# Order of the first loads in a two-layer hybrid decoder kernel: x and the first weights first, parameter vectors on ScalarE's queue, late feature vectors behind the second weights

## The chip, the cores and the metric

The kernel runs on one core of a Trainium2 chip. The core has TensorE (PE, matrix products and transposes), VectorE (DVE), ScalarE (ACT), GpSimd (POOL) and SyncE (SP), each with its own instruction stream, and 16 DMA engines that carry out the transfers which SP, ACT and POOL issue. The metric is device microseconds for one execution; the time is the median of several runs. One more execution is recorded by the hardware profiler, and every duration here is read from that record.

## What is computed

The reference is a forward pass over 256 tokens of width 1024 through two layers. Only the beginning of the first layer matters here:

```python
h = rmsnorm(x, norm_mix[layer])
z = h @ w_in[layer]
cq, ckv, kpe, u_ssm, conv_a, conv_g, gates = jnp.split(z, IN_OFFSETS, axis=-1)
y_attn = mla_branch(cq, ckv, kpe, cos, sin, ...) @ w_o_attn[layer]
s = s5_branch(u_ssm, ssm_lam_re, ssm_lam_im, ssm_log_dt, ssm_b_re, ...)   # state-space branch
...
x = x + merged @ w_out[layer]
# layer 0: x + swiglu(...); layer 1: x + mixture of 8 experts, 2 per token
```

The state-space branch needs small parameter arrays (`ssm_lam_re`, `ssm_lam_im`, `ssm_log_dt`: 16 KB, 16 KB and 0.2 KB), the rotary tables need `positions` (1 KB), and norms and biases need nine feature vectors (1 to 8 KB each). The weights `w_in` come in pieces of 1 MB; x is 1 MB.

## The kernel before

Matrix products in full precision are made as three products of reduced-precision parts: a weight half `braw` (128x1024) is rounded by ACT to `bwh` (line 198), DVE subtracts to get the remainder `bwl` (line 199), and PE runs three matmuls per tile (lines 211 to 213). Where a projection is marked native, PE multiplies the raw weights directly (line 209), which needs neither split and takes longer per matmul. The projections of layer 0 run in the order of a plan: u0 (split), u1 (native), cq0 (split), then the pair conv a and g (native), gate2 (native), ckv0 (split), gate4 (native), gate0, gate5 and so on. Each 1 MB weight goes to one of two buffers (`load_next`, line 295); SP issues these loads.

Before u0 can start, x is squared and summed by ACT (line 671), DVE forms the inverse root by eight small steps (`nv`, `nr`), ACT and DVE scale one half of the tokens each into `xn` (lines 713, 714), PE transposes that sixteen times (line 731), and ACT and DVE split the result into `aH` and `aL` (lines 201, 202), scaled by `fv`, the feature vectors turned by a transpose (lines 387, 388). A parameter chain on DVE (`params`, from line 411) then forms tables from the transposed parameters (PE lines 426, 427 and 442): exponentials, sines, powers. It feeds the rotary table `tk` (PE line 517), the state-space output tables `rn` and `mout`, and input tables `ab`, which need the loads of `ssm_b_re` and `ssm_b_im` that ACT issues (line 602).

Three things set the order. The source gives a program order; a compile-time scheduler reorders each engine's stream within the dependences; on the chip each engine then runs its stream strictly in order. Transfers issued by SP and ACT count on eight shared completion semaphores, and a transfer that takes one again waits until the earlier transfer on it has landed: SP's third load waits for x in this way. In `mixer` (line 871) the old code issues x in `setup`, then the parameters (`params`, up to its first `yield`), then the feature vectors (`feature_rows`: the first two on SP, seven on ACT), and the first weight load comes when `top_up` asks for it.

Of the kernel before, what the change touches and what calls it, by code (L numbers as in the profile page):

```python
# [81 lines left out]
class Prog:  # L82
# [279 lines left out]


    def feature_rows(self):
        nc, io = self.nc, self.io
        spec = [("norm_mix", 8), ("norm_ffn", 8), ("q_norm", 2), ("kv_norm", 1), ("ssm_d", 4),
                ("ssm_b_glu", 4), ("conv_b", 4), ("conv_ln_g", 4), ("conv_ln_b", 4)]
        rows = [self.mixp.tile([128, 128], F32, tag=t, name="frows", bufs=1) for t in ("wr", "P1")]
        self.col = {}
        r = 0  # L370
        for name, n in spec:
            first = r < 32
            (nc.sync if first else nc.scalar).dma_start(
                rows[0][r:r + 2 * n] if first else rows[1][r - 32:r - 32 + 2 * n],
                io[name].rearrange("l (c p) -> (l c) p", p=128))
            for l in range(DEPTH):
                self.col[name, l] = r + l * n
            r += 2 * n
        self.nf = r
        self.fv = self.cp.tile([128, r], F32, name="fv")  # L380
        return rows

    def features(self, rows, ps, i):
        nc = self.nc
# [26 lines left out]
    def params(self, ps):  # L411

        nc, io = self.nc, self.io

        rows = self.scratch([64, 128])
        dtr = self.scratch([32, 2])
        pos_i = self.scratch([2, 128], I32)
        nc.sync.dma_start(rows[:32], io["ssm_lam_re"].rearrange("l (c g) p -> (l c) (g p)", g=2))
        nc.sync.dma_start(rows[32:], io["ssm_lam_im"].rearrange("l (c g) p -> (l c) (g p)", g=2))
        nc.sync.dma_start(dtr, io["ssm_log_dt"].rearrange("l (c g) -> (l c) g", g=2))  # L420
        nc.sync.dma_start(pos_i, io["positions"].rearrange("b (t p) -> (b t) p", p=128))
        yield 0
        dte = self.scratch([32, 2, 64])
# [1 line left out]
        p = ps.tile([128, 512], F32, name="aux", bufs=self.naux)  # L425
# [82 lines left out]
        for j in range(2):  # L508
            c, s = cs[:, 0, 32 + 16 * j:48 + 16 * j], cs[:, 1, 32 + 16 * j:48 + 16 * j]
# [361 lines left out]
    def mixer(self, l, wk, psp, raw=None):  # L871
        nc, io = self.nc, self.io
        if l == 0:
            params = self.params(psp)
            next(params)
            rows = self.feature_rows()
        if l == 0:
            xn = self.norm_stats(wk)
            self.features(rows, psp, 0)
# [6 lines left out]
            hH, hL = lambda c: H[:, c], lambda c: Lo[:, c]  # L886
        if l == 0:
            self.top_up()
            self.features(rows, psp, 1)
            for _ in params:  # L890
                pass
        mmt = lambda: psp.tile([128, 2, 256], F32, name="mm", bufs=2)
        aux = lambda: psp.tile([128, 512], F32, name="aux", bufs=1)

# [1101 lines left out]
```

## Time and profile before

| | us |
|---|---|
| median of 3 runs | 1732.92 (1732.33 to 1732.94) |
| the profiled execution | 1734.29 |
| its span, first to last instruction | 1732.6 |
| around the span | 1.69 |
| PE busy in the span | 1693.9 |
| mean granted TensorE clock | 0.994 |

PE is the busiest engine by far. Its idle time is therefore the thing to look for: where it sits, what ended it, and whether it stands at the beginning, where the change acts. Matmuls are pipelined, so the start of one to the start of the next is the time that one costs.

### The profile page before, as it was taken

The page shows a single profiled execution, that of the slowest core. Times are in us where ns is not written, and L with a number is a line of the kernel's source. Part 1 is how long each engine was busy: PE and PEld are TensorE (multiplying, and loading weights), DVE is VectorE, ACT ScalarE, POOL GpSimd, SP SyncE. Part 2 cuts the span into 40 slices and gives each one's busy share as a digit, 9 for nine tenths or more (in the row PEclk, how much of TensorE's full clock was granted, in tenths as well). Part 3 has the DMA queues.
Part 4 walks back from the last instruction along what each step waited for, and adds up shares of the span by engine and source line. Part 5 has one row for each costly group of instructions (what it writes and reads, how often), then busy time and mean ns, then how long its engine had stood idle before and what let it go on. Part 6 is the DMA issues. An engine that isn't in the chain of part 4 may idle for free.

```text
span 1732.6 us, 26103 instructions
## 1 busy us (share of the span) xinstructions
PE 1693.9 (98%) x9721; PEld 1458.9 (84%) x9721; DVE 1467.7 (85%) x2161; ACT 1170.1 (68%) x1534; POOL 44.9 (3%) x64
## 2 busy tenths in 40 slices
PE   7999999999999999999999999999999999999997
PEld 6899898999989999888888888888788888888875
DVE  7878887855578998689999999898988998989897
ACT  4545555664453665568887887787877887878775
POOL 2000000000000000000000000000000000100020
PEclk9999999999999999989999999999999999999999
DMA  5523355645644746679999799699999899998993
GB/s 157 150 82 99 117 182 177 176 147 182 195 147 153 242 147 221 235 279 378 362 369 395 274 383 395 250 394 395 342 393 393 299 393 392 340 394 320 395 394 140
DMA packets 262311, 471.27 MB, mean 272 GB/s; under 512 B 26832, under 2 KB 104816, under 8 KB 262176
## 3 DMA queue, kind: packets, MB, share of 16 engines
q1 hardware_dynamic: 245124, 455.70, 73.6%
q10 hardware_dynamic: 14732, 5.79, 1.3%
q0 software_dynamic: 2320, 8.03, 1.3%
q8 instruction: 78, 1.28, 0.3%
q14 instruction: 57, 0.47, 0.1%
HBM read 463.70 MB, written 5.78 MB: 271 GB/s over the span
## 4 chain that ended last, share of the span: by engine, by line
PE 93%; DVE 3%; ACT 2%; DMA 1%; issue 1%; ACTq 0%; SPq 0%; DVEq 0%
PE mm L212 19%; PE mm L211 19%; PE mm L213 19%; PE Y L212 6%; PE Y L213 6%; PE Y L211 6%; PE acc L213 2%; PE acc L212 2%; PE acc L211 2%; PE tr L1790 1%; PE mm L209 1%; PE bu L1237 1%; PE spare L629 1%; DVE bwl L199 1%; ACT bwh L198 1%
## 5 line engine op out<-in xcount | busy, mean ns | idle before, releaser
L198 ACT ACTIVATE bwh<-braw 128x1024 fp32r<-128x1024 f32 x248 | 261.1, 1058 | 201.5 <-PE mm L212 126.5
L199 DVE TENSOR_TENSOR bwl<-braw,bwh 128x1024 fp32r<-128x1024 f32 x248 | 301.4, 1223 | 103.5 <-ACT bwh L198 96.0
L211 PE MATMUL mm<-bwh,bxm 128*128 128x512 f32 x672 | 266.2, 396 | 0.0
L212 PE MATMUL mm<-bwl,bxm 128*128 128x512 f32 x672 | 264.6, 394 | 1.2 <-DVE bwl L199 1.2
L213 PE MATMUL mm<-bwh,bxm 128*128 128x512 f32 x672 | 262.5, 391 | 0.0
L212 PEld LDWEIGHTS mm<-bwl,bxm 128*128 128x128 f32 x672 | 126.3, 188 | 33.4 <-DVE bwl L199 9.4
L211 PE MATMUL mm<-aH,bwh 128*128 128x256 f32 x512 | 148.8, 291 | 0.4 <-ACT bwh L198 0.4
L213 PE MATMUL mm<-aH,bwl 128*128 128x256 f32 x512 | 146.4, 286 | 2.6 <-DVE bwl L199 2.6
L213 PEld LDWEIGHTS mm<-bwh,bxm 128*128 128x128 f32 x672 | 126.1, 188 | 25.9
L211 PEld LDWEIGHTS mm<-bwh,bxm 128*128 128x128 f32 x672 | 126.2, 188 | 25.2
L212 PE MATMUL mm<-aL,bwh 128*128 128x256 f32 x512 | 146.2, 286 | 0.0
L212 PE MATMUL Y<-bwl,bgates 128*128 128x512 f32 x336 | 133.5, 397 | 0.8 <-DVE bwl L199 0.8
L213 PE MATMUL Y<-bwh,bgates 128*128 128x512 f32 x336 | 132.8, 395 | 0.0
L211 PE MATMUL Y<-bwh,bgates 128*128 128x512 f32 x336 | 122.5, 400 | 0.0
L136 DVE SCALAR_TENSOR_TENSOR cacc<-zc,lc,cacc 128x256 f32<-128x256 f32 x240 | 108.7, 481 | 4.5 <-ACT cacc L1027 3.6
L211 PEld LDWEIGHTS mm<-aH,bwh 128*128 128x128 f32 x512 | 98.6, 193 | 3.8 <-issue 2.1
L213 PEld LDWEIGHTS mm<-aH,bwl 128*128 128x128 f32 x512 | 98.6, 193 | 3.1 <-DVE bwl L199 3.0
L212 PE MATMUL mm<-fL,bwh 128*128 128x256 f32 x352 | 99.4, 282 | 0.0
L213 PE MATMUL mm<-fH,bwl 128*128 128x256 f32 x352 | 99.3, 282 | 0.0
L211 PE MATMUL mm<-fH,bwh 128*128 128x256 f32 x352 | 99.3, 282 | 0.0
L212 PEld LDWEIGHTS mm<-aL,bwh 128*128 128x128 f32 x512 | 98.6, 193 | 0.2
L213 PE MATMUL mm<-baH,bxm 128*128 128x512 f32 x224 | 87.7, 391 | 0.0
(435 smaller groups left out, 4231.7 us busy)
## 6 DMA issues: line engine op xcount, KB each, us to landing
bmout<-in_moe_w SPq DMA_DIRECT2D x46, 1024.0 KB, 10.5
bbr<-in_moe_w SPq DMA_DIRECT2D x44, 1024.0 KB, 12.6
braw<-in_moe_w SPq DMA_DIRECT2D x44, 1024.0 KB, 13.9
braw<-in_w_in SPq DMA_DIRECT2D x36, 1024.0 KB, 5.3
braw<-in_ffn_w SPq DMA_DIRECT2D x31, 1024.0 KB, 5.1
bE<-in_moe_w SPq DMA_DIRECT2D x23, 1024.0 KB, 9.9
btoep<-in_moe_w SPq DMA_DIRECT2D x23, 1024.0 KB, 12.4
bq<-in_moe_w SPq DMA_DIRECT2D x23, 1024.0 KB, 14.8
```

The lines of the kernel that those rows point to most:

```text
L136: self.nc.vector.scalar_tensor_tensor(out, a, s, b, op0=op0, op1=op1)
L198: i = nc.scalar.activation(h, src, AF.Copy)
L199: j = nc.vector.tensor_tensor(l, src, h.bitcast(F32), op=OP.subtract)
L209: mm(out, wh, xh, start=start, stop=stop, skip_group_check=True)
L211: mm(out, wh, xh, start=start, stop=False, skip_group_check=True)
L212: mm(out, wh, xl, start=False, stop=False, skip_group_check=True)
L213: self.lastmm = mm(out, wl, xh, start=False, stop=stop, skip_group_check=True).ins
L629: nc.tensor.matmul(p[:, 32 * j:32 * j + 32], fx(self.bx[:, i, j]), c0m[:, i, 4 * u + j].rearrange("p a b -> p (a b)"), start=(i == 0), sto ...
L1237: nc.tensor.matmul(pb[:, i, c], self.minT[i][:, pair_at(8 * h + c)], U[:, 8 * h + c], start=True, stop=True)
L1790: nc.tensor.transpose(p[:, q * 128:(q + 1) * 128], s[:, q * 128:(q + 1) * 128], self.ident)
```

## The change

x still leads on SP. Straight behind it SP now issues the first 1 MB of weights (u0), then `positions`, then the second 1 MB (u1), then seven late feature vectors. ACT's queue, which had those seven, now issues `norm_mix`, `norm_ffn` and the three state-space parameters. The transposes of the late feature vectors come behind the parameter chain in program order.

```diff
     def feature_rows(self):
...
             first = r < 32
-            (nc.sync if first else nc.scalar).dma_start(
+            if r == 32:
+                yield rows
+            (nc.scalar if first else nc.sync).dma_start(
...
-        return rows
...
-        nc.sync.dma_start(rows[:32], io["ssm_lam_re"]...)
-        nc.sync.dma_start(rows[32:], io["ssm_lam_im"]...)
-        nc.sync.dma_start(dtr, io["ssm_log_dt"]...)
+        nc.scalar.dma_start(rows[:32], io["ssm_lam_re"]...)
+        nc.scalar.dma_start(rows[32:], io["ssm_lam_im"]...)
+        nc.scalar.dma_start(dtr, io["ssm_log_dt"]...)
         nc.sync.dma_start(pos_i, io["positions"]...)
...
     def mixer(self, l, wk, psp, raw=None):
         if l == 0:
+            self.load_next()
+            feats = self.feature_rows()
+            rows = next(feats)
             params = self.params(psp)
             next(params)
-            rows = self.feature_rows()
+            self.load_next()
+            for _ in feats:
+                pass
...
             self.top_up()
-            self.features(rows, psp, 1)
             for _ in params:
                 pass
+            self.features(rows, psp, 1)
```

The scheduler answers with other streams on every engine. From instruction 1036 of PE's 13450, 537 of DVE's and 194 of ACT's on, the order is that of before. Line numbers of the changed kernel are up to 7 higher. Three places matter.

On ACT, from the sum of squares on (`junk`): the names are as above, `h` is the unsplit copy for native projections. Before, then after:

```order
L671 ACT_TABLE_LOAD
L671 ACTIVATE junk,ss<-x 128x512 x4
L713 ACTIVATE xn<-x,nr 128x256 x2
L713 ACTIVATE xn<-x,nr 128x512
L201 ACTIVATE aH<-hp,fv 128x256
L198 ACTIVATE bwh<-braw 128x1024
L201 ACTIVATE aH<-hp,fv 128x256 x4
L198 ACTIVATE bwh<-braw 128x1024
```

```order
L422 DMA scr<-in_ssm_log_dt 32x2
L673 ACT_TABLE_LOAD
L673 ACTIVATE junk,ss<-x 128x512 x4
L198 ACTIVATE bwh<-braw 128x1024 x2
L715 ACTIVATE xn<-x,nr 128x256 x2
L715 ACTIVATE xn<-x,nr 128x512
L201 ACTIVATE aH<-hp,fv 128x256 x7
```

Both weight roundings of u0 moved ahead of `xn`.

On DVE, the end of the inverse root and what follows it (`nr` is its result):

```order
 L136 SCALAR_TENSOR_TENSOR rs_u<-rs_t 128x2
 L136 SCALAR_TENSOR_TENSOR nr<-rs_u,nr 128x2
-L388 COPY fv<-aux 128x32
-L714 TENSOR_SCALAR xn<-x,nr 128x256 x2
-L714 TENSOR_SCALAR xn<-x,nr 128x512
-L202 SCALAR_TENSOR_TENSOR aL<-hp,fv,aH 128x256
+L199 TENSOR_TENSOR bwl<-braw,bwh 128x1024
+L716 TENSOR_SCALAR xn<-x,nr 128x256 x2
+L716 TENSOR_SCALAR xn<-x,nr 128x512
+L390 COPY fv<-aux 128x32
```

The first weight remainder moved ahead of DVE's half of `xn`. The copy of `ssm_log_dt` stays in front of the whole inverse root, and the conversion of `positions` moved from its front into its middle.

On DVE again, some 50 us later, where ckv0's weights are split: `cacc` are the steps of the convolution, `ab` and `pz` products with the loaded `ssm_b_re` and `ssm_b_im`. Before, then after:

```order
L136 SCALAR_TENSOR_TENSOR zc<-mt,zc 128x2x256
L136 SCALAR_TENSOR_TENSOR cacc<-zc,lc,cacc 128x256 x5
L127 TENSOR_TENSOR ab<-lc,pz 128x1024
L136 SCALAR_TENSOR_TENSOR cacc<-zc,lc,cacc 128x256
L199 TENSOR_TENSOR bwl<-braw,bwh 128x1024 x2
```

```order
L136 SCALAR_TENSOR_TENSOR zc<-mt,zc 128x2x256
L136 SCALAR_TENSOR_TENSOR cacc<-zc,lc,cacc 128x256
L127 TENSOR_TENSOR ab<-lc,pz 128x1024
L136 SCALAR_TENSOR_TENSOR cacc<-zc,lc,cacc 128x256
L127 TENSOR_TENSOR pz<-lc,pz 128x1024
L199 TENSOR_TENSOR bwl<-braw,bwh 128x1024 x2
```

Four convolution steps left the front of `ab`, and one 128x1024 product with `ssm_b_im` now stands ahead of the two remainders of ckv0. In the same place ACT now issues the load of `ssm_b_re` ahead of its first convolution step instead of behind it.

## Rows read from the trace of the kernel before

**Rows 1.** Busy time by stretch: length, engines, granted clock, DMA share, GB/s.

```profile
0.00:62.00 62.00, 47.64 (x265) 41.43 (x265) 45.37 (x178) 28.66 (x53) 9.89 (x37) 1.00 0.55 154
62.00:140.00 78.00, 77.44 (x612) 71.87 (x613) 64.79 (x151) 39.96 (x73) 0.00 (x0) 0.98 0.41 121
```

**Rows 2.** Timeline of SP: start, length, what it issues.

```profile
0.81 0.88 SPq L351 DMA_DIRECT2D x<-in_x  x2
...
7.50 1.05 SPq L771 DMA_DIRECT2D braw<-in_w_in  x2
```

**Rows 3.** Single microseconds of the beginning: clock, DMA share, GB/s.

```profile
3.00:4.00 1.00, 1.00 1.02 415
...
8.00:9.00 1.00, 1.00 0.57 58
...
11.00:12.00 1.00, 1.00 1.10 377
```

**Rows 4.** Packets, MB, share: SP's queue (q1), ACT's (q10), 3.5-4; q10, 5-5.5.

```profile
q1 hardware_dynamic: 63, 0.20, 100.8%
q10 hardware_dynamic: 4, 0.00, 0.9%
...
q10 hardware_dynamic: 70, 0.02, 15.8%
```

**Rows 5.** The same for 321 to 322 us, in layer 0's feed-forward part.

```profile
q1 hardware_dynamic: 87, 0.36, 97.5%
q10 hardware_dynamic: 88, 0.01, 6.0%
```

**Rows 6.** One row of the chain of waits (start, length), then two of ACT's timeline.

```profile
1.68 4.26 DMA frows<-in_ssm_d
...
5.83 0.63 ACT L671 ACTIVATE junk<-x 128x512 f32<-128x512 f32 x1 [0.45 <-DMA x<-in_x]
...
12.89 1.06 ACT L198 ACTIVATE bwh<-braw 128x1024 fp32r<-128x1024 f32 x1 [0.17 <-DMA braw<-in_w_in]
```

**Rows 7.** Timeline of DVE, in brackets its idle time before and what ended it.

```profile
7.47 1.01 DVE L424 COPY scr<-scr 32x128 f32<-32x128 f32 x1 [6.26 <-DMA scr<-in_ssm_log_dt]
...
8.47 0.23 DVE L136 SCALAR_TENSOR_TENSOR nv<-ss 128x2 f32<-128x2 f32 x1
...
10.53 1.01 DVE L714 TENSOR_SCALAR xn<-x,nr 128x256 f32<-128x256 f32 x3
...
13.98 1.23 DVE L199 TENSOR_TENSOR bwl<-braw,bwh 128x1024 fp32r<-128x1024 f32 x1 [0.74 <-ACT bwh L198]
...
20.80 0.19 DVE L131 TENSOR_SCALAR scr<-aux 128x32 f32<-128x32 f32 x1 [0.70 <-PE aux L427]
```

**Rows 8.** Timeline of PE; a native matmul counts as two (x26 is 13).

```profile
11.09 3.40 PE L731 MATMUL hp<-ident,xn 128*128 128x128 f32 x16 [1.96 <-ACT xn L713]
14.24 0.37 PE L211 MATMUL mm<-aH,bwh 128*128 128x256 f32 x1
...
23.64 5.78 PE L209 MATMUL mm<-h,braw 128*128 128x256 f32 x26
29.06 0.47 PE L211 MATMUL mm<-aH,bwh 128*128 128x256 f32 x1
...
35.00 1.46 PE L209 MATMUL mm<-h,braw 128*128 128x256 f32 x6
37.27 0.59 PE L517 MATMUL aux<-ident,tk 128*128 128x128 f32 x2 [0.81 <-DVE tk L511]
```

**Rows 9.** The chain of waits from 52 us, then PE's timeline at 59 us.

```profile
54.37 4.98 DMA pz<-in_ssm_b_re
...
59.64 0.39 PE L211 MATMUL mm<-aH,bwh 128*128 128x256 f32 x1 [0.36 <-ACT bwh L198]
...
62.18 0.58 PE L213 MATMUL mm<-aH,bwl 128*128 128x256 f32 x1 [2.03 <-DVE bwl L199]
```

**Rows 10.** Busy time and granted clock (0.50) in the three microseconds behind that wait.

```profile
62.00:65.00 3.00, 2.82 (x13) 2.82 (x14) 3.00 (x5) 0.00 (x0) 0.00 (x0) 0.50 0.86 255
```

More of the change, by code (lines that the diff above doesn't have):

```diff
@@ L417, in params @@
         pos_i = self.scratch([2, 128], I32)
-        nc.sync.dma_start(rows[:32], io["ssm_lam_re"].rearrange("l (c g) p -> (l c) (g p)", g=2))
-        nc.sync.dma_start(rows[32:], io["ssm_lam_im"].rearrange("l (c g) p -> (l c) (g p)", g=2))
-        nc.sync.dma_start(dtr, io["ssm_log_dt"].rearrange("l (c g) -> (l c) g", g=2))
+        nc.scalar.dma_start(rows[:32], io["ssm_lam_re"].rearrange("l (c g) p -> (l c) (g p)", g=2))
+        nc.scalar.dma_start(rows[32:], io["ssm_lam_im"].rearrange("l (c g) p -> (l c) (g p)", g=2))
+        nc.scalar.dma_start(dtr, io["ssm_log_dt"].rearrange("l (c g) -> (l c) g", g=2))
         nc.sync.dma_start(pos_i, io["positions"].rearrange("b (t p) -> (b t) p", p=128))
```

## Prediction

> **What bounds the kernel now.** I read the busy times first: PE is busy for 1693.9 of the 1732.6 us of the span (the table of times), so only PE's idle time, or PE at a lower clock, can be won or lost. The busy time by stretch then says where that idle time is: 14.36 of the first 62 us (62.00 less 47.64), but 0.56 of the 78 us behind them [rows 1]. All that the change moves lies in this first stretch; from PE's instruction 1036 of 13450 on the streams agree again, so whatever PE has gained or lost by then it keeps to the end. The third view, the timelines of the engines, shows what PE waited for: the normalised x (first real transpose at 11.09, first matmul of u0 at 14.24), the rotary table at 37.27, and the remainder of ckv0's weights until 62.18 [rows 8, 9]. [...]
>
> **The change part by part.** First the loads. SP's two issues of x take 0.88 us, so the first weights go out at 1.69 instead of 7.50 [rows 2]. The second half of x lands at 5.83, where ACT stops waiting for it [rows 6]; a 1.05 MB load behind it, at the 377 to 415 GB/s of the full microseconds [rows 3], takes 2.5 to 2.8 us, so I put its landing at 8.6, an estimate. Bounds: 8.3, and 10.0 if it needs the 4.2 us that it took from its first bytes (about 8.7, since the microsecond from 8 moved only 58 GB/s) to 12.89 [rows 3, 6]. So its landing is some 4.3 us earlier; that is the gain meant.
>
> What of it reaches PE? u0 needs the normalised x as well, and that is not earlier: the squares end at about 8.1, as before, since they wait for x. Behind them three things stand in the way. (a) `ssm_log_dt` is now the fifth issue on ACT, at about 2.3. DVE's copy of it heads DVE's stream, in front of the whole inverse root. Before, its load went out behind x on SP, and the copy began at 7.47 [rows 7]. A small load issued on ACT's queue at 1.68 while x was moving landed only at 5.94 [rows 6], and the packets say why: 63 packets of SP's queue against 4 of ACT's from 3.5 to 4, and 70 of ACT's as soon as x was through [rows 4]. ACT's small loads came after what SP had issued ahead of them. Now the first weights are issued ahead of `ssm_log_dt` too. Bounds: it lands at 5.9 if only x holds it, at 8.7 behind the first weights, at 11.5 (8.7 and another 2.8) if the second weights hold it as well. I take 8.7, by the row that is nearest.
>
> [...]
>
> (b) With the copy at 8.7 and a small operation's 0.23 us [rows 7] the inverse root begins at 8.95 instead of 8.47 (9.7 if the copy again takes its 1.01). It took 2.06 to 10.53 [rows 7] and now has the conversion of `positions` within, 0.2: it ends at 11.2. `positions` is issued behind the first weights and lands with them, in time. (c) DVE then makes the first weight remainder before its half of `xn`: start to start that is some 1.14 (1.23 less an overlap of 0.09 with its neighbour) [rows 7]. So `xn` begins on DVE at 12.35, 1.8 later than before. ACT's two roundings, 1.06 each from 8.6, end at 10.7 and cost nothing, covered by the wait for the root; were the weights to land at 10.0 they would end at 12.1 and cost nothing still. PE's stream now begins with the second piece of `xn`: from about 12.9, and 15 of its 16 transposes at (14.24 less 11.09)/16 = 0.197 us [rows 8] make the first matmul of u0 15.85. **That is 1.6 later than 14.24.**
>
> Second, u0 and u1. Before, from 14.24 to 23.64 PE needed 9.40 us for 48 matmuls that come every 0.124 when nothing holds them (29.06 to 35.00, all 48 of cq0) [rows 8], since it waited for remainders and fitted 3 matmuls of u1 and four transposes between. Now both weight halves are split early: 48 x 0.124 = 5.95, three transposes 0.53, and about 0.2 for each of two changes of operand kind, 6.9. u0 ends at 22.75. u1's 16 native matmuls at (29.06 less 23.64)/13 = 0.417 [rows 8] make 29.4 against 29.06: **0.35 late**, so 1.25 of the 1.6 comes back.
>
> Third, the parameter chain. Its transposes stand earlier in PE's stream, behind 16 matmuls: its start on DVE is at 15.85 + 1.9 + 0.6 = 18.35 instead of 20.80 [rows 7]. From there to the first transpose of `tk` it took 16.5 (37.27 less 20.80) [rows 7, 8], and one `aL` of 0.4 has come in: 35.3. But that transpose has moved forward as well, to within cq0, where PE arrives at 29.4 + 39 x 0.124 = 34.2, so PE waits 1.1 where it waited 0.81. What is then left of the work that was done at 37.86 before: the pair of transposes and a change 0.8, nine matmuls 1.1, three natives 1.3, the late feature vectors 0.25, together 3.45. That makes 38.75: **0.9 late**.
>
> Fourth, ckv0. PE would arrive 0.9 later, but it waits there anyway, so DVE decides. `ssm_b_re` is now issued ahead of ACT's convolution step, right after `mt`: not 54.37 but about 53.5 (PE ends the 16 natives ahead of `mt` at about 59.28 less the 16 of gate2, 6.7, which is 52.6, and is 0.9 late). With its 4.98 [rows 9] it lands at 58.5; if the load of ckv0's weights holds it as long as before, at 60.2. Before, the remainder was ready 2.8 after `ab` began, at 59.35. Now the product with `ssm_b_im` stands between, 1.14 more: 3.9, so PE goes on at 62.4 to 64.1 instead of 62.18. I take the middle and a little less, **1.0 late**, and with it the same low clock behind the wait. The four convolution steps moved behind, 4 x 0.4, and the remainders of gate0 now behind the tables cost nothing as long as PE has 13 natives and 90 transposes and small matmuls to run meanwhile; where that cover ends, up to 1.5.
>
> The sum against the profiled execution is 1734.29 + 1.0 = 1735.3. That execution is 1.37 above the median, so the forecast is 1732.92 + 1.0 = **1733.9**.
>
> **The rivals.** *`ssm_log_dt` lands with x* (5.9). The root begins at 8.1, all of the above up to `tk` is 0.85 earlier, PE's delay at 37.86 turns into a lead of nearly nothing, and ckv0 gives -0.6 to +1.1: 1732.9. For it speak [rows 5], against it [rows 4].
>
> *`ssm_log_dt` lands behind both weights* (slower). If ACT's small packets wait until SP's stream has a gap, DVE stands until 11.5, the root starts 2.8 later than in the forecast, and nothing in the parameter chain can give it back: 1733.9 + 2.8 = 1736.7. From a landing at 11.2 on it is slower by over 0.2%. Against it: the second weights wait for a semaphore that x frees, so they are issued after it, and in [rows 4] a queue's turn went by who was first.
>
> *The wait for ckv0's remainder disappears* (faster). If `ssm_b_re`, issued earlier, lands before 57, the remainder is there when PE comes, and the 0.36 + 2.03 us go, and with them the low clock, where 13 matmuls took 2.82 [rows 10] instead of 13 x 0.124: 1.2. That is -3.6, with a start between -0.4 and +0.9: 1728.9 to 1730.2. Against it: the load took 4.98 beside ckv0's own weights, and DVE has an operation more to do.
>
> *Nothing arrives at PE*: the streams differ but every wait ends where it did, 1732.9.
>
> **How the numbers follow.** About 0.2%, 3.5 us, is what a measurement of this kernel can tell from no change. Chances: forecast 0.45 (its own range 1732.9 to 1735.8), `ssm_log_dt` with x 0.27 (1731.5 to 1734.0), behind both weights 0.08, the wait gone 0.08, of which 0.05 lies beyond 0.2%, nothing arrives 0.12. So faster 0.05, within 0.2% 0.87, slower 0.08. The range 1731.0 to 1736.0 takes in the forecast, the first rival and the last, and leaves out the two at the ends.
>
> **What would show it.** In the changed profile: the first `bwh` at about 8.6 and not 12.89; DVE's copy of `ssm_log_dt` at 8.7, `nv` at 8.95, DVE's `xn` at 12.35, the first u0 matmul at 15.85; no wait of PE for `bwl` in u0; the first transpose of `tk` at 35.3 after a wait of about 1.1; the wait for ckv0's `bwl` ending between 62.4 and 64.1 and the clock at 0.50 behind it. The forecast is wrong if the copy starts near 6 or near 11.5, if `ssm_b_re` lands before 57, or if PE shows new waits over 1.5 us between 65 and 200.

## The result, and the profile after

The changed kernel takes 1743.18 us (median of six runs, 1741.41 to 1744.86) where the kernel before, run beside it, takes 1734.23: **1.0052 times as long, 95% interval 1.0041 to 1.0063**. It is 9 us slower, and the prediction, 1733.9 with a range up to 1736.0, did not hold. One execution of e1 below took 5931 us and is left out of its figures. The profiled execution took 1744.22 with a span of 1742.4.

The busy times by stretch, in the columns of [rows 1], show where to look. First the kernel after, then the stretch from 140 us on of before, which [rows 1] did not reach:

```profile
0.00:62.00 62.00, 47.43 (x265) 41.77 (x265) 42.37 (x174) 28.57 (x53) 9.84 (x37) 1.00 0.53 150
62.00:140.00 78.00, 75.35 (x595) 69.79 (x596) 65.42 (x153) 39.74 (x73) 0.00 (x0) 0.98 0.39 118
140.00:175.00 35.00, 34.02 (x252) 31.07 (x251) 23.92 (x64) 12.78 (x24) 4.24 (x8) 0.85 0.25 75
```

```profile
140.00:175.00 35.00, 34.78 (x275) 31.03 (x274) 29.43 (x90) 18.12 (x41) 4.25 (x8) 1.00 0.21 63
```

The first 62 us, where the prediction looked for everything, differ by 0.2 us of busy time. From 62 to 140 PE idles 2.1 us more. From 140 to 175 it is nearly as busy as before but finishes 23 matmuls fewer, at a mean granted clock of 0.85: that place stands in no part of the prediction.

A ledger makes this exact. PE does the same work in both kernels, so the same group of matmuls can be looked up in both traces; how much later it starts is what has been lost by then. The columns are single profiled executions (the experiments are told below).

| place in before's trace, us | what starts there | after | e1 | e2 | e8 | e12 |
|---|---|---|---|---|---|---|
| 62.18 | ckv0, behind the wait | +1.69 | +1.78 | +0.12 | +0.10 | +0.10 |
| 120.60 | `aux<-u`, second half | +2.05 | +2.20 | +0.18 | -0.94 | +0.30 |
| 154.25 | `aux<-ys`, first half | +2.27 | +2.41 | +0.19 | -0.94 | +0.29 |
| 162.96 | `aux<-ys`, second half | +6.60 | +2.41 | +4.10 | -0.95 | +1.80 |
| 191.96 | `mm<-br` | +8.58 | +2.81 | +4.92 | -0.51 | +2.75 |
| 212.95 | `mm<-br` | +9.51 | +3.46 | +5.84 | +0.22 | +2.56 |
| 357.45 | `spare<-c0m` | +10.60 | +4.29 | +6.42 | +1.04 | +3.12 |
| 1719.09 | `aux<-bgates`, last stage | +9.85 | +3.30 | +6.53 | +1.48 | +2.30 |

So after is 2 us late when the first state-space tables are through, and 6.3 us more go between 154 and 192. The rest is small; part of it is again a lower clock, behind the wait for `ssm_c_im` near 302 us (0.86 from 300 to 312 in e1 and e2, 1.00 in before and after) and from 357 us on in after (0.55 from 357 to 360). A lower clock comes in one execution and not in another (0.68 from 158 to 174 in after, 1.00 in e5, the same kernel again), so a column of this table holds some microseconds of chance.

**The beginning** went nearly as predicted. Rows of after that answer to [rows 7], [rows 6] and [rows 8], on DVE, ACT and PE:

```profile
8.05 0.42 DVE L426 COPY scr<-scr 32x128 f32<-32x128 f32 x1 [6.84 <-DMA scr<-in_ssm_log_dt]
8.55 0.16 DVE L136 SCALAR_TENSOR_TENSOR nv<-ss 128x2 f32<-128x2 f32 x1
...
11.64 1.01 DVE L716 TENSOR_SCALAR xn<-x,nr 128x256 f32<-128x256 f32 x3
```

```profile
9.41 2.00 ACT L198 ACTIVATE bwh<-braw 128x1024 fp32r<-128x1024 f32 x2 [0.89 <-DMA braw<-in_w_in]
```

```profile
15.59 0.53 PE L211 MATMUL mm<-aH,bwh 128*128 128x256 f32 x1
...
29.33 0.47 PE L211 MATMUL mm<-aH,bwh 128*128 128x256 f32 x1
...
35.51 0.30 PE L519 MATMUL aux<-ident,tk 128*128 128x128 f32 x1 [1.16 <-DVE tk L513]
```

**At ckv0** (answering to [rows 9]) PE goes on at 63.87 instead of 62.18. Its two waits in after, then DVE ahead of them in after, then in before:

```profile
60.80 0.39 PE L211 MATMUL mm<-aH,bwh 128*128 128x256 f32 x1 [0.70 <-ACT bwh L198]
...
63.87 0.58 PE L213 MATMUL mm<-aH,bwl 128*128 128x256 f32 x1 [2.56 <-DVE bwl L199]
```

```profile
59.92 1.23 DVE L127 TENSOR_TENSOR ab<-lc,pz 128x1024 f32<-128x1024 f32 x1 [0.94 <-DMA pz<-in_ssm_b_re]
61.07 0.48 DVE L136 SCALAR_TENSOR_TENSOR cacc<-zc,lc,cacc 128x256 f32<-128x256 f32 x1
61.46 1.22 DVE L127 TENSOR_TENSOR pz<-lc,pz 128x1024 f32<-128x1024 f32 x1
62.60 2.35 DVE L199 TENSOR_TENSOR bwl<-braw,bwh 128x1024 fp32r<-128x1024 f32 x2
```

```profile
60.51 0.48 DVE L136 SCALAR_TENSOR_TENSOR cacc<-zc,lc,cacc 128x256 f32<-128x256 f32 x1
60.91 2.35 DVE L199 TENSOR_TENSOR bwl<-braw,bwh 128x1024 fp32r<-128x1024 f32 x2
63.18 0.48 DVE L136 SCALAR_TENSOR_TENSOR cacc<-zc,lc,cacc 128x256 f32<-128x256 f32 x1
63.57 1.22 DVE L127 TENSOR_TENSOR pz<-lc,pz 128x1024 f32<-128x1024 f32 x1
```

The second product (`pz`) has come ahead of the remainders (`bwl`) that PE is waiting for.

**At 160 us** the same has happened in another place. `P` holds the state-space branch's outgoing states, which the `y` matmuls take. In after, its last operation stands behind the bias additions `u`, which themselves wait 1.48 us for PE's transposes; in before it stood ahead. DVE after, then before:

```profile
156.86 0.69 DVE L127 TENSOR_TENSOR P<-P,T 128x512 f32<-128x512 f32 x1
159.02 0.87 DVE L136 SCALAR_TENSOR_TENSOR u<-u,fv,aux 128x256 f32<-128x256 f32 x2 [1.48 <-PE aux L1327]
159.81 0.68 DVE L127 TENSOR_TENSOR P<-P,wi 128x512 f32<-128x512 f32 x1
```

```profile
154.59 0.69 DVE L127 TENSOR_TENSOR P<-P,T 128x512 f32<-128x512 f32 x1
155.19 0.69 DVE L127 TENSOR_TENSOR P<-P,wi 128x512 f32<-128x512 f32 x1
156.75 0.48 DVE L136 SCALAR_TENSOR_TENSOR u<-u,fv,aux 128x256 f32<-128x256 f32 x1 [0.88 <-PE aux L1320]
```

PE has two `y` matmuls that need no final `P`, and then stands. Two microseconds after it has gone on, its matmuls lengthen (each counts as two). PE after, then its busy time and clock around this place:

```profile
159.18 0.39 PE L1254 MATMUL y<-P,mout 128*128 128x63 f32 x2
160.55 0.43 PE L1255 MATMUL y<-P,mout 128*128 128x63 f32 x2 [0.98 <-DVE P L127]
...
162.38 0.39 PE L1254 MATMUL y<-P,mout 128*128 128x63 f32 x2
162.61 0.51 PE L1255 MATMUL y<-P,mout 128*128 128x63 f32 x2
```

```profile
158.00:174.00 16.00, 15.02 (x100) 13.28 (x98) 7.01 (x23) 4.75 (x12) 4.24 (x8) 0.68 0.12 33
```

Single two-microsecond stretches of after show a granted clock of 0.50 from 164 to 172, 0.68 in the stretch before and 0.76 behind. So the 6.3 us between 154 and 192 are, by difference, the wait, 1.2 with what surrounds it (e5 below, which has the wait alone, loses 1.19 between the two `aux<-ys`), 0.4 up to 192 that e1 and e5 lose as well at clock 1.00 (0.40 and 0.43), and some 4.7 of half clock.

### The profile page after: what moved, and what is told of

Read it like the earlier page. It is cut to its first block, busy times and chain, and to the rows that moved or that the text cites. A ratio compares the mean times of both kernels' runs of the same rounds, so it can differ in the third digit from the quotient of the medians.

```text
span 1742.4 us, 26100 instructions
## 1 busy us (share of the span) xinstructions
PE 1700.8 (98%) x9721; PEld 1464.8 (84%) x9721; DVE 1466.8 (84%) x2161; ACT 1171.0 (67%) x1534; POOL 44.8 (3%) x64
## 4 chain that ended last, share of the span: by engine, by line
PE 92%; DVE 4%; ACT 2%; DMA 2%; issue 1%; ACTq 0%; SPq 0%; DVEq 0%
PE mm L212 19%; PE mm L211 19%; PE mm L213 19%; PE Y L212 6%; PE Y L213 6%; PE Y L211 6%; PE acc L213 2%; PE acc L212 2%; PE acc L211 2%; PE tr L1797 1%; PE mm L209 1%; DVE bwl L199 1%; ACT bwh L198 1%; PE bu L1244 1%; PE spare L631 1%
```

## The experiments

Theory A: what counts is not the loads but the order that the builder gave VectorE because of them, at two places where PE waits for it, together with the low clock behind such a wait. Rivals: the low clock belongs to the narrow matmuls there (B), or the loss is the beginning's and only shows up later (C). All ratios are to the kernel before in runs on the same chip. "Pin" means an issue-order edge between two instructions of one engine, with no wait.

**The order at P, undone and done alone.** e1 is the changed kernel with `P` ahead of `u`; e2 is the kernel before with the opposite pin.

```diff
# e1, in turn_out of the changed kernel
-                tt(hi, hi, wi, OP.add)
+                last = tt(hi, hi, wi, OP.add)
+                if h and l == 0:
+                    for q in range(2):
+                        self.tc.add_manual_dep(sg["bias", 0, q].ins, last.ins.name, ...)
...
# e2, in turn_out of the kernel before
-                tt(hi, hi, wi, OP.add)
+                if h and l == 0:
+                    with self.tc.issue_after(sg["bias", 0].ins):
+                        tt(hi, hi, wi, OP.add)
+                else:
+                    tt(hi, hi, wi, OP.add)
...
```

> The changed kernel with one pin: in layer 0 VectorE issues the last addition of the second state half's outgoing rotation (the write of P, which TensorE's y matmuls wait for) ahead of the first half's two bias additions (u), as it stood in the kernel before. Theory A (of the 9 us, 5.9 come from this order: 1.0 us in which TensorE waits for P at 160 us, and 4.9 us at a granted clock of 0.50 behind it): no wait of TensorE for P, granted clock 1.00 from 150 to 190 us, time 5 to 6.5 us below the changed kernel, 1737 to 1738 where before stands at 1734.2. Rival B (the low clock comes from what TensorE does there, narrow matmuls and transposes, and not from the wait): the wait goes, the low clock stays, 1742 to 1743. Rival C (the 9 us were lost at the beginning and the later places only follow): 1743.

> The kernel before with the opposite pin and nothing else of the change: the write of P is issued behind the two bias additions. Theory A: TensorE waits 1.0 to 2.0 us for P near 158 us, the granted clock falls to 0.50 for some 10 us behind that, time 4.5 to 7 us above before (1739 to 1741 where before stands at 1734.2). Rivals B and C: a wait of about 1 us without a lower clock, or no effect: 1734 to 1735.5.

e1: 1.0026 (1.0015 to 1.0036), 1737.0 beside 1732.5. e2: 1.0037 (1.0024 to 1.0051), 1740.8; six of its eight executions lie between 1740.6 and 1741.2, the other two at 1736.2 and 1737.7. Busy time and clock of 158 to 174 us, e1 and then e2, and e2's wait on PE:

```profile
158.00:174.00 16.00, 15.39 (x127) 13.43 (x124) 11.91 (x44) 9.22 (x25) 4.25 (x8) 1.00 0.15 41
```

```profile
158.00:174.00 16.00, 15.36 (x99) 13.29 (x99) 9.34 (x32) 7.52 (x19) 4.25 (x8) 0.79 0.04 4
```

```profile
158.46 0.43 PE L1248 MATMUL y<-P,mout 128*128 128x63 f32 x2 [0.98 <-DVE st L131]
```

In e1 the `y` matmuls are the same and run at clock 1.00, with no wait; in e2, which has no part of the change, both the wait and the low clock appear (the profile names DVE's neighbouring `st`, but the write of `P` is what ends at 158.4). B and C fall for this place. The price is a little under what I had written for e1: half of the 9 us, not two thirds.

**Which part of the change makes the order.** e3 calls the two weight loads early and changes nothing else; e4 has the other parts without that.

```diff
# e3, in mixer of the kernel before
+            self.load_next()
             params = self.params(psp)
             next(params)
             rows = self.feature_rows()
+            self.load_next()
# e4: the queue lines of the change's diff, and
-            self.features(rows, psp, 1)
             for _ in params:
                 pass
+            self.features(rows, psp, 1)
```

> The kernel before with one part of the change alone: the two weight loads are called ahead of and right behind the parameters' loads, on the queue that they had; feature vectors and parameters stay on their queues. The builder then orders VectorE around 160 us as in the changed kernel. Theory A: the low clock at 160 us is there, time 6 to 10 us above before (1740 to 1744). Rival C (the queues and the late feature vectors cost most): within 2 us of before.

> The kernel before with the other two parts: parameters and early vectors on ScalarE's queue, late vectors on SyncE's, and the late vectors' transposes behind the parameters'; the weight loads are called where they were. VectorE's order around 160 us stays that of before. Theory A: no low clock at 160 us, time from 1 us below to 1.5 us above before (1733 to 1736). Rival C: most of the 9 us, 1740 to 1743.

e3: 1.0051 (1.0036 to 1.0067); e4: 1.0010 (1.0000 to 1.0020). The early call of the weight loads alone brings a loss as large as the whole, and the order at `P` and the 0.98 us wait with it (until 162.10). But its profile shows clock 1.00 there, against what I expected, and its loss is in part another: e3 is 3.20 late at ckv0 already, where after is 1.69 late, since its small loads now stand behind the weights on SP's queue (feature vectors at PE at 11.34 instead of 8.85, transposes of x at 13.42 instead of 11.09).

**Is the low clock always there?** e5 is the changed kernel again; e9 lengthens e2's wait by pinning `P` behind the next product (`lt`) too.

> The changed kernel once more, for a second profile of it. Theory A in its present form: the wait of TensorE for P at 160 us (0.98 us) stands in every execution, since it comes from the order of the program, and the low clock behind it (4.7 us lost in the first profile) in most executions but not in all: the times fall into two groups, near 1741.5 and near 1744.5. Rival D (the low clock belongs to the place, not to chance): the same low clock at the same place, 5 to 6 us, and one group of times.

> The kernel before with the write of P pinned behind the first GELU product (lt) as well as behind the bias additions: the wait of e2_before_sub_last made longer. Theory A: TensorE waits 2.3 to 3.0 us for P near 158 us instead of 0.98; the low clock behind a wait of this length comes in nearly every execution, as behind the 1.6 to 2.6 us waits at ckv0: time 6.5 to 9 us above before (1739 to 1742 where before stands at 1732.6), one group of times. Rival D (the low clock there has nothing to do with how long TensorE waited): 2 us above e2_before_sub_last and the same two groups.

e5: 1.0048 (1.0034 to 1.0061), in two groups (1738.8 to 1740.8, and 1743.1 and 1743.5). The same wait, and this time no low clock behind it:

```profile
161.57 0.43 PE L1255 MATMUL y<-P,mout 128*128 128x63 f32 x2 [0.98 <-DVE P L127]
```

```profile
158.00:174.00 16.00, 14.80 (x133) 12.78 (x131) 11.08 (x37) 7.58 (x19) 4.24 (x8) 1.00 0.20 60
```

So the low clock at `P` is not certain, as the expectation of e5 said. e9 did not do what I wanted: the builder drew the attention's `sc` matmuls forward, and PE waited twice (0.78 and 0.68) instead of once for longer. Its profile has no low clock there and was its fastest execution (1736.5); the others lie between 1739.0 and 1744.1 at mean granted clocks of 0.992 to 0.988. Ratio 1.0042 (1.0030 to 1.0054). Whether a longer wait makes the low clock surer stays open at this place.

**The order at ckv0.** e6 gives the changed kernel before's order at both places. e8 puts ckv0's remainders ahead of all products, e12 does so without e1's pin, and e7 does it in the kernel before.

```diff
# e7, e8, e12, in ssm_inp (self.kv: the remainders of ckv0's two halves)
...
+            pin = (lambda: self.tc.issue_after(self.kv[0])) if l == 0 else nullcontext
-            self.tt(ab[:, o], fr, x, OP.mult)
+            with pin():
+                self.tt(ab[:, o], fr, x, OP.mult)
             yield 1.1
-            self.tt(tmp, fi, y, OP.mult)
+            with pin():
+                self.tt(tmp, fi, y, OP.mult)
# e6: kv[1], and the first ab product left free
```

> The changed kernel with two pins, so that VectorE keeps the order of before at both places: P ahead of the bias additions at 160 us (as e1_sub_first), and both rounding remainders of ckv0's weights (bwl, L199) ahead of the second product of the input matrices' build (pz, L127) at 61 us. Theory A: TensorE goes on with ckv0 at 62.6 instead of 63.9 us, 1.0 to 1.5 us less than e1_sub_first, that is 1 to 3 us above before (1733.5 to 1735.5 where before stands at 1732.5). Rival E (the time gained at ckv0 is waited for again at the input matrices' transposes, 74 to 87 us, whose chain on VectorE then ends later): within 0.5 us of e1_sub_first, 1737.

> The kernel before with one pin: both remainders of ckv0's weights go on VectorE ahead of all products of the input matrices' build. In the trace of before the first remainder starts at 60.9 us, 1.4 us after its rounding has ended (59.5), behind a 1.22 us product and a cacc addition. Theory A (order on VectorE at the places where TensorE waits is what counts): TensorE's wait of 2.0 us there falls to about 0.9 us and the time to 1 to 3 us below before (1729.5 to 1731.5 where before stands at 1732.5; the larger figure if the low clock behind the wait goes too). Rival E: the products come 1.5 to 2.3 us later, TensorE waits for their transposes from 68 us on, and the time is that of before within 0.5 us or up to 2 us longer.

> The changed kernel with P ahead of the bias additions and both remainders of ckv0's weights ahead of all products of the input matrices' build. Theory A: 1.5 to 3 us less than e1_sub_first, near before (1732 to 1735 where before stands at 1732.5). Rival E: within 0.5 us of e1_sub_first, 1737.

> The changed kernel with ckv0's remainders pinned ahead (as e8_after_kv_first) but with P left behind the bias additions: the fourth corner beside the changed kernel (neither pin), e1_sub_first (P alone) and e8_after_kv_first (both). If the two places add up (theory A): the wait of 0.98 us for P is there, ckv0's two waits are 0.9 and 1.0 us as in e8_after_kv_first, and the time is 3 to 5 us above e8_after_kv_first, 1.0020 to 1.0035 times before (some 1736.5 to 1739 where before stands at 1733). If P's cost hangs on the late ckv0: near e8_after_kv_first, 1.0005 to 1.0012.

| kernel | P ahead of u | ckv0's remainders first | ratio to before (95%) |
|---|---|---|---|
| after; e5 | no | no | 1.0052 (1.0041 to 1.0063); 1.0048 (1.0034 to 1.0061) |
| e1 | yes | no | 1.0026 (1.0015 to 1.0036) |
| e12 | no | yes | 1.0027 (1.0015 to 1.0038) |
| e8 | yes | yes | 1.0007 (0.9998 to 1.0016) |

The two places add up, as far as the intervals can tell. `P` ahead is worth 0.0020 to 0.0024, some 3.5 to 4.2 us; ckv0's remainders first 0.0019 to 0.0023, some 3.3 to 4.0. Each of these prices is a difference of two ratios and good to about 2.5 us, an estimate from their intervals; the two together, e5 less e8 on one chip, are 0.0041, 7.1 us. With both pins, the loads moved as the change moves them cost 1.2 us, which the interval does not tell from nothing. PE's waits at ckv0 in e8, and the clock of 60 to 70 us in e8 and in e12:

```profile
60.80 0.38 PE L211 MATMUL mm<-aH,bwh 128*128 128x256 f32 x1 [0.91 <-ACT bwh L198]
...
62.28 0.39 PE L213 MATMUL mm<-aH,bwl 128*128 128x256 f32 x1 [0.97 <-DVE bwl L199]
```

```profile
60.00:70.00 10.00, 8.23 (x61) 7.81 (x62) 10.00 (x14) 4.44 (x8) 0.00 (x0) 1.00 0.71 212
```

```profile
60.00:70.00 10.00, 8.22 (x51) 7.95 (x52) 10.00 (x14) 3.43 (x7) 0.00 (x0) 0.83 0.71 211
```

The waits are the same in both to 0.02 us (0.93 and 0.97 in e12), yet e12 has the low clock behind them and e8 has not; by 120.60 that is 1.24 us between them in the ledger.

e6 went against theory A: 1.0037 (1.0023 to 1.0051), no better than e1. PE went on at 62.94, 0.9 earlier than after, but then stood 1.21 us until 97.81 for `U` and was 3.2 late at 154. That is the kind of loss that its rival E names, though at another place and larger. So the order of before at these two places does not bring its time back by itself: with these pins a wait came up elsewhere. e7 missed as well: 0.9998 (0.9989 to 1.0007). With the products held back, the builder put further `cacc` additions in front of the remainders, which started at 60.67 instead of 60.91; nothing was left to gain.

**Does the beginning count?** e10 is e8 with the norm's products ahead of the first weight split. e11 is e4 with e7's pin, as a candidate for a faster kernel.

```diff
# e10, in top_up, for u0's first half
+                    with self.tc.issue_after(self.last[0]), self.tc.issue_after(self.last[1]):
+                        self.ready.append((key,) + self.wsplit(src))
```

> The kernel of e8_after_kv_first with the norm's products (xn) ahead of the first rounding of the weights on both ScalarE and VectorE, which undoes the prediction's step (c) at the beginning. If the beginning counts: first transposes near 11.2 instead of 12.3 us and 0.5 to 1 us less at the end (1734 where e8_after_kv_first had 1734.8). If it is hidden, as the parameters' chain on VectorE (tk, 35.3 us) holds TensorE next: the gain is waited for at tk, whose wait grows from 1.16 to about 1.5 us, and the time is that of e8_after_kv_first within 0.5 us.

> The kernel of e4_queues_only (no weight load led) with both remainders of ckv0's weights ahead of the products of the input matrices' build. VectorE keeps the order of before at 160 us. Theory A: TensorE's waits at ckv0 (0.77 and 1.39 us in e4_queues_only) fall together by 0.3 to 0.8 us, no wait for P; 1731 to 1733.5 where before stands at 1732.6, a version that may equal or beat both. Rival E: as e4_queues_only, 1733 to 1735.

e10: 1.0010 (1.0001 to 1.0018), 1735.0 where e8 had 1734.8. The transposes of x start at 11.44, 0.57 earlier than in e8, and the first transpose of `tk` at 35.78, no earlier than e8's 35.30: the beginning is hidden. e11: 1.0008 (0.9999 to 1.0016), 1734.7, as its rival E said: the waits at ckv0 fell from 2.16 to 1.84, but PE came to them 1.6 later. No version beat the kernel before.

## Why the prediction was wrong

**The loads: near in time, not in kind.** The first rounding came at 9.41, within the bounds 8.3 to 10.0 (8.6 taken). The copy of `ssm_log_dt` came at 8.05 (8.7 taken). The first rival, a landing at 5.9, fell. But the load did not come behind the first weights either: it was there after x (second half at 6.29) and before them. Packets of the two queues in after from 5 to 5.5 us, then from 2.8 to 8:

```profile
q1 hardware_dynamic: 111, 0.20, 101.5%
q10 hardware_dynamic: 1, 0.00, 0.1%
...
q1 hardware_dynamic: 1138, 1.83, 96.6%
q10 hardware_dynamic: 207, 0.05, 4.6%
```

In each half microsecond from 5.5 to 7.5 ACT's queue moved 32 to 41 packets beside 154 to 172 of SP's. So its small loads came in between the weights, and that 8.05 lies so near 8.7 is partly luck. The reading of [rows 4] on which 8.7 rested, that ACT's small loads come after what SP issued ahead of them, did not hold for the first weights.

**u0, u1 and the parameter chain: right, in part by luck.** First matmul of u0 at 15.59 (15.85), end of u1 at 29.33 (29.4), `tk` at 35.51 after a wait of 1.16 (35.3 and 1.1). Two errors offset each other on the way: DVE's `xn` began at 11.64, 0.7 ahead of the forecast, and from the first transpose to the first matmul of u0 PE took 3.33 (12.26 to 15.59), not 2.95. As the prediction said, the weights' landing gains nothing at PE, and e10 shows that the term (c) costs nothing at `tk` either.

**ckv0: the mechanism right, the size too small.** `ssm_b_re` landed at 59.9, within 58.5 to 60.2, and `pz` stood between, as said. But I took "the middle and a little less" of 62.4 to 64.1, and PE went on at 63.87: +1.69, not +1.0. The term that was too small is the load: 6.2 us from its issue (53.72) to its use (59.92), where [rows 9] had 4.98. I also let the delay end there. Behind it the chain `ab` to `bx` was late too, and PE waited 0.33, 0.23 and 0.22 for `bx` to transpose where before it waited 0.23 once: +2.05 by 120 us. The runs priced this order at 3.3 to 4.0 us. That is more than the late restart alone: by 120 us PE was 0.94 ahead of before in e8, whose profile has no low clock at ckv0, and 0.30 behind in e12, which has it.

**The step that failed** is the last of the fourth part: remainders and additions moved behind "cost nothing as long as PE has" cover and "where that cover ends, up to 1.5". With it falls the premise of the first part, "All that the change moves lies in this first stretch": the first stretch ends at 62 us, and the changed streams go on to some 217 us on PE and 235 us on DVE in after. I compared PE's stream and the few places on DVE around the loads, and did not follow DVE's changed order to its end; the exchange of `u` and `P` stands in it before any run. In place of "nothing, up to 1.5" the runs showed 3.5 to 4.2 us for this exchange: a wait of 0.98, and behind it, in after's profile, some 4.7 us of half clock. The price of one place was wrong as well: 1.5 allowed for the wait, but not for a new stretch at half clock behind a wait. Even the sign that the prediction named for its own failure, "new waits over 1.5 us between 65 and 200", would not have found it: the wait was 0.98.

**Chances and range.** "Slower" had 0.08, all of it on `ssm_log_dt` behind both weights. That an order changed by the builder puts a wait where there was none should have been a rival of its own, since [rows 1] showed a stretch with only 0.56 us of idle time in 78: a stream so closely filled can lose more than it can win. Nor did the range allow for the scatter of one and the same kernel: before itself ran from 1730.6 to 1740.0 beside e1 to e4, at mean granted clocks of 0.995 and 0.989.

## What to carry to other kernels

When a compile-time scheduler orders the engines, moving a load by some microseconds is an edit of every stream behind it: compare the whole order of each engine that PE waits for, and look for an operation that PE needs and that now stands behind one that waits for PE. Two such exchanges on VectorE cost some 7 to 8 us here; the loads themselves moved the time by about 1 us, if at all. Where the bound engine has hardly any idle time, pin the order at such a place before judging the change itself, and read the whole trace again: pins at both places took away nearly all of the loss in e8, while slightly looser ones in e6 brought a wait elsewhere.

## What the runs showed of the hardware

**A short wait of PE may cost far more than itself, and not each time.** A single wait of 0.98 us at `P` was followed by a lower granted clock in two of five profiled executions (0.50 from 164 to 172 us in after, a mean of 0.79 from 158 to 174 in e2; 1.00 from 158 to 174 in e3, e5 and e12), some 4.7 and 3.1 us of loss. In before, e1, e8, e10 and e11, where PE did not wait there, the clock stayed at 1.00 (158 to 174 us, in e10 and e11 150 to 180); in e9, with two waits of 0.78 and 0.68, it did too. Two of five against none of five would be little by itself, but the mean clocks of all executions point the same way: averaged over a kernel's executions they are 0.9912 to 0.9931 in the six with a wait at `P` (after, e2, e3, e5, e12 and e9), and 0.9932 to 0.9943 in the eight without. From 60 to 70 us, around ckv0's waits, PE idled 2.03 to 3.42 us in before, after, e1, e2, e3, e5 and e9, and the mean clock was 0.66 to 0.83 in all seven; of four with 1.43 to 1.84 us idle, e10 and e12 show 0.83, e8 and e11 1.00. Near 302 us, behind the wait for `ssm_c_im` (2.78 us in before, 2.10 in after until 311.18, 2.14 in e12), the clock was 0.86 from 300 to 312 us in e1, e2, e3, e5, e8, e9 and e12 and 0.83 from 300 to 310 in e11, but 1.00 in before, after (311 to 325) and e10, though the wait was longer in before than in e12. The same program can go either way: after and e5 have the same 0.98 us at `P`, and mean clocks of 0.68 and 1.00 from 158 to 174 us. In after the clock goes with the two groups of times: the three executions near 1744.5 have a mean granted clock of 0.990 to 0.991, the three near 1741.5 one of 0.992 to 0.993. It does not account for all scatter: e11's executions all have 0.994 and lie between 1733.2 and 1737.2. What decides it was not settled.

**A part of the loss is neither idle time nor clock.** From 192 to 213 us after, e1 and e2 lose 0.65 to 0.93 us with no more idle time (0.63 us in before, 0.65 in after) and a clock of 1.00. The same 24 matmuls of `aux<-ident,sm`, `sc` and `cln` take 3.79 us from start to start in after and 3.03 in before. The order around them differs, but a price for each change between kinds of matmul does not explain it: in before they stand in 9 groups between the others, in after in 8, and cost less. The cause stays open.
